# Weight buffers of their own for the merge gates, the first pair's loads beside the attention gate, and the casts of the late weights' high parts on ScalarE

## The chip, the core and the metric

The kernel runs on one core of a Trainium2 chip. The core has a matrix engine (TensorE, "PE" in the profile, with the loading of its weights as "PEld"), VectorE ("DVE"), ScalarE ("ACT"), GpSimd ("POOL"), and a sync engine ("SP") that in this kernel issues every transfer between HBM and the on-chip memory. Each engine works through its own instructions in order and waits at semaphores for the others. The metric is the device time of one execution in microseconds (us).

## The reference

One inference step of a decoder layer: a prompt of 1024 tokens and eight single tokens, 1032 columns in all, go through one combined projection into two gated branches, whose sum is projected once more. Cut to what matters here:

```python
def project(x, c, pos, p):
    h = rmsnorm(x, p['g_pre']) * (1 + scale) + shift
    z = h @ p['w_in']
    zq, zkv, zg, za, zconv, zcg, zm = jnp.split(z, ...)
...
def finish(x, o_attn, conv_out, pr, p):
    ya = (o_attn * jax.nn.silu(pr['a_gate'])) @ p['w_br_a']
    yb = (pr['cb'] * conv_out * jax.nn.silu(pr['cgate'])) @ p['w_br_b']
    ga, gb = jnp.split(jax.nn.sigmoid(pr['merge']), 2, axis=-1)
    o = (ga * ya + gb * yb) @ p['w_out']
    return x + pr['gate'] * rmsnorm(o, p['g_post'])
```

`a_gate` (`za`, 512 columns of `w_in`) is the attention gate, `merge` (`zm`, 2048 columns) the merge gates of the two branches. The width of the model is 1024, that of the branches 512.

## The kernel before

**Arithmetic.** Each float32 operand of a matmul is split in two parts: a high part, cast to TensorE's own 32-bit type, and a low part, which is the rest. A product takes three matmuls: high by high, high by low, low by high. `Hh` and `Hl` are the parts of the normed input, `wh` and `wl` those of a weight. Tokens run along the free dimension, 1032 of them: in thirds of 344 (`CH`) in the projections and in quarters of 258 (`HS`) in the merge gates.

**Weights.** The class `Weights` (object `W`) holds a list of weight tiles of 128x512, the items, in the order of their use. `load` brings an item into `wraw`, `do_split` casts it to `wh` (line 182, through `copy`, lines 110 or 112) and makes `wl` (line 183, through `sub`, line 115); `get` hands the pair out. Each of the three has three buffers, so an item can be split as soon as the third one before it is released by the last matmul that reads it. `W.hi` and `W.lo` name the engine of the two steps: at first `W.hi` is ScalarE (`A`); line 1109, at the end of attention, puts both on VectorE (`V`).

**Stages, in order of time in the trace.** The attention and its filling work end near 583 us. The last quarter of the convolution (`conv_tiles(3, ...)`, loop with `YH` and `YL`) follows to 635. Then comes branch b's projection `yb`, eight items by three thirds, to 690 (loop at line 1303; its results go to HBM in `ybd`). The attention gate (loop `for j in range(4)`, `e_za`) takes 690 to 735.3: eight items of `W`; ScalarE makes a tanh (line 1351) and the high part `oh`, VectorE multiplies and makes `ol`, and both go to HBM in `oad`. Beside it VectorE makes sums of the input's halves for the stage after (`sums14`, line 1335). The merge gates, eight pairs of 128-column blocks, run from 735.3 to 918, then branch a's projection to 964 (here `w_out` comes in as `wor` and is split to `WOh` and `WOl`), and the output to 1069.

**The merge gates.** A pair (class `Pair`) takes the 2x2 products of blocks of weights and input by a scheme with seven products in place of eight: the operands are a11, a12, a22 as loaded and the sums s1 = a21 + a22, s2 = s1 - a11, s3 = a11 - a21, s4 = a12 - s2. `load` brings the four blocks of 256 KB into buffers `ra` (six of them, in the pool `gsp`, line 1400), `total` makes the sums on VectorE into `wraw` (lines 1263 and 115), `prepare` makes `wh` on ScalarE and `wl` on VectorE, and `product` issues 24 matmuls, 12 for each half of 258 columns. a11's results are copied to `c1` by ScalarE, VectorE adds them to those of s2 and s3 (`u2`, `u3`, line 1263), and sums on VectorE and a tanh on ScalarE (`sgo`, line 1494) end it. Pair 0's a11 and a12 are the last items of `W`, loaded and split ahead. `Gate` objects, two behind each pair, use `ra` too, for blocks of `w_ada`. The eight loads of `M` bring `ybd` back.

**What sets the order.** The code's order is that of the functions; a scheduler then orders the instructions of each engine by its own estimate of when they can run, so rows of one engine stand in another order than the code. All transfers go through SP's one queue, which issues them in that order and stops where one has to wait. Pools stand on two sides of the on-chip memory, `left` and `right`, as stacks: a pool that is opened takes the place of one that was closed, and its first writers wait for the last readers of what lay there. `gsp` opens at line 1373, after the gate's pool `tp` is closed; pools that opened before it stay below.

## Time and profile before

| | us |
|---|---|
| three runs | 1069.9, 1070.4, 1072.63 |
| median | 1070.4 |
| profiled execution, its own time | 1071.21 |
| its span in the trace | 1069.2 |
| TensorE busy | 1021.5 |
| VectorE busy | 727.9 |
| ScalarE busy | 545.6 |

The profile is of one execution; its span is 2.0 us shorter than that execution's own time, and 0.8 us of that time is what it lies above the median of the runs. Times in the trace count from the span's start. Engines overlap, so the busy times don't add up to the span. In a timeline a row can stand for several like instructions (xN), and what stands in brackets is how long the engine was idle ahead of it and what ended that. Matmuls are pipelined: the time of one is longer than the distance between two.

### The profile page before, as it was taken

How to read it: one execution, taken by the hardware profiler on the slowest of the kernel's cores; microseconds unless marked ns; L12 is line 12 of the kernel's file. 1: busy time of each engine (PE TensorE's matmuls, PEld its weight loads, DVE VectorE, ACT ScalarE, POOL GpSimd, SP SyncE). 2: the span in 40 equal slices, each digit the busy share in tenths (PEclk: the TensorE clock that was granted, in tenths of full speed). 3: DMA queues.
4: the chain of work that ended last, by engine and by line, in shares of the span. 5: the costliest groups of instructions: out<-in, count | busy, mean ns of one | idle time of the engine just before them, and what ended most of it. 6: DMA issues, size and time to landing. Idle time of an engine off the chain costs nothing.

```text
span 1069.2 us, 18057 instructions
## 1 busy us (share of the span) xinstructions
PE 1021.5 (96%) x6526; PEld 940.3 (88%) x6526; DVE 727.9 (68%) x1920; ACT 545.6 (51%) x1198; POOL 94.0 (9%) x98
## 2 busy tenths in 40 slices
PE   5899999989999999999999999997899999999997
PEld 4689999978888888988898999997899999997786
DVE  4677656458887888878888748494666676785433
ACT  4566533347888877888777214232344444222221
POOL 2100000122232112220111010000000000000000
PEclk9899999989999999999999999999899999999999
DMA  9752243210111011010101363345734422873222
GB/s 315 232 145 84 62 103 77 77 45 22 35 30 26 16 25 30 21 30 11 26 11 44 98 199 115 114 142 167 237 109 120 119 70 100 264 224 113 80 79 78
DMA packets 117178, 104.15 MB, mean 97 GB/s; under 512 B 25443, under 2 KB 101674, under 8 KB 117090
## 3 DMA queue, kind: packets, MB, share of 16 engines
q1 hardware_dynamic: 117090, 103.02, 32.6%
q8 instruction: 51, 0.84, 0.3%
q14 instruction: 37, 0.30, 0.1%
HBM read 79.13 MB, written 21.76 MB: 94 GB/s over the span
## 4 chain that ended last, share of the span: by engine, by line
PE 77%; DVE 10%; ACT 4%; issue 2%; DMA 1%; SPq 1%; POOL 1%; POOLq 0%; DVEq 0%; ACTq 0%
PE psacc L106 36%; PE psS L106 23%; PE psO L106 6%; PE psT L106 5%; PE psT L1016 5%; DVE P L961 2%; DVE P L987 2%; ACT P L966 1%; DVE pl L115 1%; SPq L91 1%; DMA ra<-w_in 1%; ACT ph L110 1%; PE psT L1028 1%; DVE sm L975 1%; PE psT L570 1%
## 5 line engine op out<-in xcount | busy, mean ns | idle before, releaser
L106 PE MATMUL psacc<-Hh,wh 128*128 128x344 f32 (+1 forms) x816 | 262.0, 321 | 4.1 <-DVE Hh L112 3.8
L106 PE MATMUL psacc<-Hl,wh 128*128 128x344 f32 (+1 forms) x816 | 258.0, 316 | 0.9 <-DVE ss L329 0.7
L106 PE MATMUL psacc<-Hh,wl 128*128 128x344 f32 (+1 forms) x816 | 257.3, 317 | 0.1
L106 PEld LDWEIGHTS psacc<-Hh,wh 128*128 128x128 f32 x816 | 154.2, 189 | 12.9 <-DVE Hh L112 3.9
L106 PEld LDWEIGHTS psacc<-Hl,wh 128*128 128x128 f32 x816 | 154.1, 189 | 6.0 <-DVE Hl L115 2.6
L106 PEld LDWEIGHTS psacc<-Hh,wl 128*128 128x128 f32 x816 | 153.5, 189 | 2.4 <-DVE wl L115 1.1
L966 ACT ACTIVATE P<-P,mx 128x64 f32<-128x64 f32 (+5 forms) x192 | 115.1, 600 | 34.7 <-DVE mx L961 33.1
L115 DVE TENSOR_TENSOR pl<-psT,ph 128x512 fp32r<-128x512 f32 x132 | 90.4, 687 | 24.5 <-ACT ph L110 24.1
L110 ACT ACTIVATE wh<-wraw 128x512 fp32r<-128x512 f32 x94 | 58.8, 627 | 84.8 <-PE psS L106 37.1
L1016 PE MATMUL psT<-ident,P 128*128 128x128 f32 x528 | 89.9, 280 | 9.1 <-DVE P L987 7.1
L115 DVE TENSOR_TENSOR wl<-wraw,wh 128x512 fp32r<-128x512 f32 x98 | 67.3, 688 | 41.3 <-ACT wh L110 39.7
L110 ACT ACTIVATE ph<-psT 128x512 fp32r<-128x512 f32 x132 | 77.9, 591 | 28.6 <-PE psT L1016 24.6
L961 DVE CUSTOM_DVE_ANT_0 P<-psS,kbig 128x64 f32<-128x64 f32 (+4 forms) x192 | 74.2, 407 | 20.2 <-PE psS L106 19.4
L1016 PEld LDWEIGHTS psT<-ident,P 128*128 128x128 f32 x528 | 63.7, 141 | 26.9 <-DVE P L987 10.7
L106 PE MATMUL psS<-K,qh 128*128 128x384 f32 (+6 forms) x208 | 67.4, 327 | 2.2 <-DVE mx L961 1.2
L106 PE MATMUL psS<-K,ql 128*128 128x384 f32 (+6 forms) x208 | 68.3, 329 | 0.0
L115 POOL TENSOR_TENSOR wl<-wraw,wh 128x512 fp32r<-128x512 f32 x28 | 37.1, 1326 | 275.5 <-ACT wh L110 263.4
L106 PE MATMUL psO<-pl,V 128*128 128x512 f32 x132 | 60.8, 461 | 0.0
L106 PE MATMUL psO<-ph,V 128*128 128x512 f32 x132 | 52.4, 397 | 0.0
L961 DVE CUSTOM_DVE_ANT_0 P<-psS,kbig,mx 128x256 f32<-128x256 f32 (+3 forms) x80 | 41.9, 524 | 9.4 <-PE psS L106 8.2
L106 PEld LDWEIGHTS psS<-K,qh 128*128 128x128 f32 x208 | 39.4, 189 | 4.9 <-DMA qh<-qh 1.3
L1613 POOL TENSOR_TENSOR fst<-fst,mhalf 128x1 f32<-128x1 f32 (+1 forms) x9 | 4.9, 549 | 422.5 <-DVE fst L1612 422.5
(392 smaller groups left out, 2351.3 us busy)
## 6 DMA issues: line engine op xcount, KB each, us to landing
wraw<-w_in SPq DMA_DIRECT2D x46, 256.0 KB
ra<-w_in SPq DMA_DIRECT2D x32, 256.0 KB
ybd<-yb SPq DMA_DIRECT2D x24, 172.0 KB
M<-ybd SPq DMA_DIRECT2D x8, 516.0 KB
sgd<-sgo SPq DMA_DIRECT2D x8, 516.0 KB
OA<-oad SPq DMA_DIRECT2D x6, 688.0 KB
sg<-sgd SPq DMA_DIRECT2D x8, 516.0 KB
x<-x_prompt SPq DMA_DIRECT2D x8, 512.0 KB
```

Of the source, the lines that this page charges most:

```text
L91: return nc.sync.dma_start(out, in_)
L106: PE.matmul(out, lhsT, rhs, start=start, stop=stop, skip_group_check=True)
L110: A.activation(out, in_, AF.Copy)
L115: eng.tensor_tensor(out=out, in0=a, in1=b, op=OP.subtract)
L570: PE.transpose(pt[:, t * 128:(t + 1) * 128], raw[:, (t0 + t) * 128:(t0 + t + 1) * 128], ident)
L961: V.tensor_tensor_reduce(out=Pb[:, j, o:o + n], in0=ps[:, c0:c0 + n], in1=m, scale=1.0, scalar=init, op0=OP.add, op1=OP.min, accum_out=mx[ ...
L966: A.activation(Pb[:, j, 0:total_n], Pb[:, j, 0:total_n], AF.Exp, bias=mx[:, j, ci % 2:ci % 2 + 1], scale=-1.0, accum_out=sm[:, 0, x, j:j + 1])
L975: V.tensor_tensor(out=fac, in0=fac, in1=gt_[:, b0:b0 + np_, :], op=OP.mult)
L987: V.tensor_scalar(p, p, f[:, jj:jj + 1], None, op0=OP.mult)
L1016: PE.transpose(pt[:, j * 128:(j + 1) * 128], u.P[u.br][:, j, n * 128:(n + 1) * 128], ident)
L1028: PE.transpose(pt[:64, j * 128:(j + 1) * 128], u.P[0][:, j, :], ident)
L1613: P.tensor_tensor(out=st[:n, 3:4], in0=st[:n, 3:4], in1=mhalf[:n], op=OP.pow)
```

## The change

It does three things.

- Line 1109 sets `W.lo` alone. `W.hi` stays what it was in attention, ScalarE, so the casts of the high parts of all later items of `W` are ScalarE's: the last of the convolution, branch b, the attention gate, a11 and a12 of pair 0, and branch a. By the counts of instructions, 32 casts `wh<-wraw` leave VectorE.
- The `ra` buffers, six as before, move from the pool `gsp` to a pool `rap` of their own, which opens ahead of the gate's pool `tp`. `Gate.prepare` takes its tile from there too.
- The loads of pair 0 are written ahead of the loop of the attention gate (`raw0`); those of the other pairs stay where they were.

```diff
--- before.py
+++ after.py
@@ -1106,7 +1106,7 @@
         product()
     for _ in filler:
         pass
-    W.lo, W.hi = V, V
+    W.lo = V
     actx.close()
     att.close()
 
@@ -1322,6 +1322,19 @@
 
     tsp4 = pool("tsp4", "left", tsctx)
     T4 = [tsp4.tile([128, 4, HT], F32R, name=f"T4{x}") for x in "hl"]
+    rap = pool("rap", "left", tsctx)
+
+    def raw_tile():
+        return rap.tile([128, 4, 128], F32, name="ra", tag="ra", bufs=6)
+
+    def load_raw(c0):
+
+        raw = {}
+        for x, i, kh in (("a11", 0, 0), ("a21", 1, 0), ("a22", 1, 1), ("a12", 0, 1)):
+            raw[x] = raw_tile()
+            dma(raw[x], w_in[:, 4 * kh:4 * kh + 4, c0 + 128 * i:c0 + 128 * i + 128])
+        return raw
+
     tctx = ExitStack()
     tp = pool("tp", "left", tctx)
     zt = {x: [tp.tile([128, CH], d, name=x, tag=x, bufs=b) for _ in range(b)] for x, d, b in
@@ -1345,6 +1358,7 @@
             yield
 
     making = sums14()
+    raw0 = load_raw(GA0)
     for j in range(4):
         def e_za(c, acc, cs):
             t, oh, ol = spare("zt", F32, 3), spare("oh", F32R, 2), spare("ol", F32R, 2)
@@ -1379,9 +1393,6 @@
     def gtile(name, n, bufs):
         return fresh[name].pop(0) if fresh[name] else gp.tile([128, n], F32, name=name, tag=name, bufs=bufs)
 
-    def operand(c0, kh):
-        return w_in[:, 4 * kh:4 * kh + 4, c0:c0 + 128]
-
     RIGHT = {"a11": lambda k: quarter(k, 0), "a12": lambda k: quarter(k + 4, 0), "s1": lambda k: quarter(k, 1),
              "s4": lambda k: quarter(k + 4, 1)}
     for n, t in (("s2", T2), ("s3", T3), ("a22", T4)):
@@ -1395,10 +1406,7 @@
             self.raw, self.ops = {}, {}
 
         def load(self):
-            c0 = (GB0 if self.gb else GA0) + 128 * self.f
-            for x, (i, kh) in (("a11", (0, 0)), ("a21", (1, 0)), ("a22", (1, 1)), ("a12", (0, 1))):
-                self.raw[x] = gp.tile([128, 4, 128], F32, name="ra", tag="ra", bufs=6)
-                dma(self.raw[x], operand(c0 + 128 * i, kh))
+            self.raw = load_raw((GB0 if self.gb else GA0) + 128 * self.f) if self.n else raw0
 
         def total(self, x):
             if x in self.raw:
@@ -1504,7 +1512,7 @@
             self.b, self.k = n // KT, n % KT
 
         def prepare(self, q):
-            r = gp.tile([128, 512], F32, name="ra", tag="ra", bufs=6)
+            r = raw_tile().rearrange("p k c -> p (k c)")
             dma(r, wada[:, self.k, 2048 + 512 * self.b:2560 + 512 * self.b])
             h = wp.tile([128, 512], F32R, name="wh", tag="wh", bufs=3)
             l = wp.tile([128, 512], F32R, name="wl", tag="wl", bufs=3)
```

What it does to the order of SP's queue, first in the kernel before, around the end of the attention gate (`oad` are the gate's writes; `M` the loads for later pairs; `ra_8603` to `ra_8609` pair 0's blocks; `ra_8653` and `ra_8655` the first two of pair 1):

```order
L91 DMA oad1_7410<-ol_8521 128x344 [waits DMAHW0_49,DVE_49]
L91 DMA M_8585<-ybd_7412 128x1032 [waits DMAHW1_49,DVE_49,PE_49]
L91 DMA oad0_7409<-oh_8563 128x344 [waits DMAHW2_49,Activation_49]
L91 DMA oad1_7410<-ol_8564 128x344 [waits DMAHW3_49,DVE_49]
L91 DMA M_8585<-ybd_7412 128x1032 [waits DMAHW4_49]
L91 DMA M_8585<-ybd_7412 128x1032 [waits DMAHW5_49]
L91 DMA ra_8603<-w_in 128x4x128 [waits DMAHW6_49,PE_49]
L91 DMA ra_8605<-w_in 128x4x128 [waits DMAHW7_49]
L91 DMA ra_8607<-w_in 128x4x128 [waits DMAHW0_49]
L91 DMA ra_8609<-w_in 128x4x128 [waits DMAHW1_49]
L91 DMA ra_8653<-w_in 128x4x128 [waits DMAHW2_49]
L91 DMA ra_8655<-w_in 128x4x128 [waits DMAHW3_49]
```

Here pair 0's four blocks and two of pair 1 stand behind the gate's last writes and three loads of `M`. In the changed kernel, around the end of branch b and the start of the gate (`ybd` are branch b's last writes, `wraw` the gate's items; `ra_8081` to `ra_8087` are pair 0's blocks, `ra_8656` and `ra_8658` the first two of pair 1):

```order
L91 DMA ybd_7412<-yb_8013 128x344 [waits DMAHW0_49,Activation_49]
L91 DMA ybd_7412<-yb_8033 128x344 [waits DMAHW1_49,Activation_49]
L91 DMA ra_8081<-w_in 128x4x128 [waits DMAHW2_49,PE_49]
L91 DMA ra_8083<-w_in 128x4x128 [waits DMAHW3_49]
L91 DMA ybd_7412<-yb_8049 128x344 [waits DMAHW4_49,Activation_49]
L91 DMA ra_8085<-w_in 128x4x128 [waits DMAHW5_49]
L91 DMA ra_8087<-w_in 128x4x128 [waits DMAHW6_49]
L91 DMA wraw_8179<-w_in 128x4x64 [waits DMAHW7_49,DVE_49]
L91 DMA wraw_8179<-w_in 128x4x64 [waits DMAHW0_49]
L91 DMA ra_8656<-w_in 128x4x128 [waits DMAHW1_49]
L91 DMA ra_8658<-w_in 128x4x128 [waits DMAHW2_49]
```

These six blocks now stand between branch b's last writes and behind the gate's first item. And the changed kernel at the end of the gate, where SP had three loads of `M` ahead of pair 0's (`ra_8660` and `ra_8662` are the last two of pair 1):

```order
L91 DMA oad0_7409<-oh_8574 128x344 [waits DMAHW7_49,Activation_49]
L91 DMA ra_8660<-w_in 128x4x128 [waits DMAHW0_49,DVE_49]
L91 DMA oad1_7410<-ol_8575 128x344 [waits DMAHW1_49,DVE_49]
L91 DMA ra_8662<-w_in 128x4x128 [waits DMAHW2_49]
L91 DMA ra_8788<-w_ada 128x512 [waits DMAHW3_49,DVE_49]
L91 DMA M_8596<-ybd_7412 128x1032 [waits DMAHW4_49]
L91 DMA M_8596<-ybd_7412 128x1032 [waits DMAHW5_49]
L91 DMA M_8596<-ybd_7412 128x1032 [waits DMAHW6_49]
```

So six of the first eight blocks have moved from behind the gate to ahead of it; the other two stand around the gate's last write, and `M` stands behind them and behind a block of `w_ada`.

ScalarE around the end of the gate, before (`zt` is the gate's tanh, `oh` its high part, `c1` the copies of a11's results, `wh_8615` the high part of s2, `wh_8649` of s3, `wh_8687` of s1):

```order
L110 ACTIVATE Hh_87<-t1_8077 128x516 [waits PE_49]
L1351 ACTIVATE zt_8562<-psacc_8529 128x344 [waits PE_49]
L1354 ACTIVATE oh_8563<-zt_8562 128x344 [waits DMAHW5_49,DVE_49,Activation_49]
L110 ACTIVATE c1_8592<-psacc_8619 128x258 [waits PE_49,Activation_49]
L110 ACTIVATE c1_8593<-psacc_8620 128x258 [waits PE_49]
L1494 ACTIVATE sgo_8590<-psacc_8619 128x258 [waits DMAHW3_49,DMAHW2_49,DMAHW4_49,DMAHW0_49,DMAHW6_49,DVE_49,PE_49]
L1494 ACTIVATE sgo_8590<-psacc_8620 128x258 [waits PE_49]
L110 ACTIVATE wh_8615<-wraw_8611 128x512 [waits DVE_49]
L110 ACTIVATE wh_8649<-wraw_8647 128x512 [waits DVE_49]
L110 ACTIVATE wh_8687<-wraw_8612 128x512
```

The three high parts of pair 0's sums stand behind `c1` and the first two `sgo`. ScalarE there in the changed kernel (`wh_8569` belongs to a12 of pair 0, `wh_8618` to s2, `wh_8652` to s3, `wh_8690` to s1):

```order
L1368 ACTIVATE oh_8531<-zt_8530 128x344 [waits DMAHW1_49,DVE_49,Activation_49]
L110 ACTIVATE wh_8569<-wraw_8442 128x512 [waits DMAHW2_49,PE_49]
L110 ACTIVATE Hh_87<-t1_8080 128x516 [waits PE_49]
L110 ACTIVATE wh_8618<-wraw_8614 128x512 [waits PE_49]
L1365 ACTIVATE zt_8573<-psacc_8540 128x344 [waits PE_49]
L1368 ACTIVATE oh_8574<-zt_8573 128x344 [waits DMAHW3_49,DVE_49,Activation_49]
L110 ACTIVATE wh_8652<-wraw_8650 128x512 [waits DVE_49,PE_49]
L110 ACTIVATE wh_8690<-wraw_8615 128x512 [waits PE_49,Activation_49]
L110 ACTIVATE c1_8603<-psacc_8622 128x258
L110 ACTIVATE c1_8604<-psacc_8623 128x258
L1502 ACTIVATE sgo_8601<-psacc_8622 128x258 [waits DMAHW2_49,DMAHW1_49,DMAHW4_49,DMAHW0_49,DMAHW6_49,DVE_49,PE_49]
```

The high part of s2 has moved from behind the first `sgo` to ahead of the gate's last tanh, and those of s3 and s1 to ahead of `c1`; the one of s1 waits for a buffer that TensorE leaves.

VectorE at the same place, before (`wraw_8612` is s1's sum, `wraw_8611` s2's, `wraw_8647` s3's, `wraw_8749` s4's):

```order
L1352 SCALAR_TENSOR_TENSOR zt_8562<-zt_8562,psacc_8529 128x344 [waits Activation_49]
L115 TENSOR_TENSOR Hl3_418<-t1_8077,Hh_87 128x516
L1353 TENSOR_TENSOR zt_8562<-zt_8562,QO_871 128x344 [waits DVE_49]
L1355 SCALAR_TENSOR_TENSOR ol_8564<-zt_8562,oh_8563 128x344 [waits DMAHW6_49,Activation_49]
L1263 TENSOR_TENSOR wraw_8612<-ra_8605,ra_8607 128x512 [waits DMAHW7_49,DMAHW0_49]
L115 TENSOR_TENSOR wraw_8611<-wraw_8612,ra_8603 128x512 [waits DMAHW6_49,DVE_49]
L115 TENSOR_TENSOR wraw_8647<-ra_8603,ra_8605 128x512
L115 TENSOR_TENSOR wl_8616<-wraw_8611,wh_8615 128x512 [waits PE_49,Activation_49]
L115 TENSOR_TENSOR wl_8650<-wraw_8647,wh_8649 128x512 [waits PE_49,Activation_49]
L115 TENSOR_TENSOR wl_8688<-wraw_8612,wh_8687 128x512 [waits PE_49,Activation_49]
L115 TENSOR_TENSOR wraw_8749<-ra_8609,wraw_8611 128x512 [waits DMAHW1_49,DVE_49]
L1263 TENSOR_TENSOR u2_8594<-psS_8691,c1_8592 128x258 [waits PE_49]
```

All of pair 0's sums and low parts stand behind the gate's last row, `ol_8564`. VectorE there in the changed kernel (s1's and s2's sums, `wraw_8615` and `wraw_8614`, stand 15 rows or more further ahead; `wraw_8867` is the first sum of pair 1):

```order
L1366 SCALAR_TENSOR_TENSOR zt_8573<-zt_8573,psacc_8540 128x344 [waits Activation_49]
L115 TENSOR_TENSOR wl_8619<-wraw_8614,wh_8618 128x512 [waits PE_49]
L1367 TENSOR_TENSOR zt_8573<-zt_8573,QO_871 128x344 [waits DVE_49]
L115 TENSOR_TENSOR wraw_8650<-ra_8081,ra_8083 128x512
L1369 SCALAR_TENSOR_TENSOR ol_8575<-zt_8573,oh_8574 128x344 [waits DMAHW4_49,Activation_49]
L115 TENSOR_TENSOR wl_8653<-wraw_8650,wh_8652 128x512 [waits PE_49,Activation_49]
L115 TENSOR_TENSOR wraw_8752<-ra_8087,wraw_8614 128x512 [waits DVE_49]
L1263 TENSOR_TENSOR wraw_8867<-ra_8658,ra_8660 128x512 [waits DMAHW0_49,DVE_49]
L115 TENSOR_TENSOR wl_8691<-wraw_8615,wh_8690 128x512 [waits PE_49,Activation_49]
L1263 TENSOR_TENSOR u2_8605<-psS_8694,c1_8603 128x258 [waits Activation_49]
L1263 TENSOR_TENSOR u2_8606<-psS_8695,c1_8604 128x258 [waits Activation_49]
```

What stood behind the gate's last multiply now stands before or between its steps; and the first sum of pair 1, which waits for a load (`ra_8660`), has come to stand ahead of s1's low part and of both `u2`.

## Rows read from the trace of the kernel before

**Rows 1.** The profile's page: busy time of each engine with its share of the span and its instructions, and the granted clock of TensorE in 40 equal slices of the span, in tenths.

```profile
PE 1021.5 (96%) x6526; PEld 940.3 (88%) x6526; DVE 727.9 (68%) x1920; ACT 545.6 (51%) x1198; POOL 94.0 (9%) x98
...
PEclk9899999989999999999999999999899999999999
```

**Rows 2.** Waits of TensorE from 575 to 735 us: engine, tile and line, what it waited for, us in total, times, longest us.

```profile
PE psacc L106 <- ACT YH L110: 0.7, 1, 0.7
PE psT L1161 <- DVE sP L1155: 0.6, 2, 0.4
```

**Rows 3.** Waits of all engines from 735 to 770 us, same columns.

```profile
DVE wraw L1263 <- DMA ra<-w_in: 10.1, 1, 10.1
...
PE psS L106 <- ACT wh L110: 9.3, 1, 9.3
...
ACT wh L110 <- DVE wraw L115: 6.7, 1, 6.7
```

**Rows 4.** The chain of waits from 735 to 770 us, in order of time: start us, us, what.

```profile
736.46 0.42 DVE zt L1352
...
738.39 0.38 ACT c L110
...
741.71 7.43 DMA ra<-w_in
...
749.17 0.70 DVE wraw L1263
...
751.26 0.04 issue
751.30 8.45 PE psS L106 x48
759.75 2.90 PE psT L106 x24
```

**Rows 5.** A table of stretches: from and to, us, then busy us (and instructions) of PE, PEld, DVE, ACT and POOL, the granted clock as a share of full, the share of the DMA engines, GB/s.

```profile
620.00:640.00 20.00, 19.32 (x133) 18.91 (x133) 7.04 (x16) 2.99 (x6) 2.78 (x3) 1.00 0.79 252
...
741.96:751.30 9.34, 0.01 (x1) 0.00 (x0) 2.00 (x4) 1.34 (x4) 0.00 (x0) 0.74 1.10 333
751.30:760.00 8.70, 8.70 (x52) 8.70 (x53) 5.77 (x11) 1.98 (x4) 0.00 (x0) 0.69 0.80 249
...
769.31:790.66 21.35, 21.35 (x174) 20.59 (x174) 12.91 (x24) 8.99 (x20) 0.00 (x0) 1.00 0.42 123
```

**Rows 6.** Timeline of SP's queue from 734 to 760 us: start us, us, engine, line, operation, out<-in, xcount.

```profile
737.98 0.32 SPq L91 DMA_DIRECT2D M<-ybd  x1
...
739.44 1.01 SPq L91 DMA_DIRECT2D M<-ybd  x2
740.54 6.59 SPq L91 DMA_DIRECT2D ra<-w_in  x6
```

**Rows 7.** Transfers issued from 690 to 800 us: out<-in, queue, operation, count, KB of one.

```profile
M<-ybd SPq DMA_DIRECT2D x8, 516.0 KB
ra<-w_in SPq DMA_DIRECT2D x16, 256.0 KB
```

**Rows 8.** Timeline of TensorE, at the end of the gate and the start of pair 0, and at the start of pair 1.

```profile
734.67 0.32 PE L106 MATMUL psacc<-Hh,wl 128*128 128x344 f32 x1
...
735.30 0.28 PE L106 MATMUL psacc<-Hh,wh 128*128 128x258 f32 x1
...
736.94 0.39 PE L106 MATMUL psacc<-Hh,wh 128*128 128x258 f32 x1
...
738.82 0.39 PE L106 MATMUL psacc<-Hh,wh 128*128 128x258 f32 x1 [0.16 <-ACT c L110]
...
769.15 0.29 PE L106 MATMUL psacc<-Hh,wh 128*128 128x258 f32 x1
```

**Rows 9.** Groups of instructions by line and shape, the casts of 128x512 weights' high parts: busy us, mean ns of one | idle us before them, and what ended most of it.

```profile
L110 ACT ACTIVATE wh<-wraw 128x512 fp32r<-128x512 f32 x94 | 58.8, 627 | 84.8 <-PE psS L106 37.1 <-PE psacc L106 25.4 <-issue 14.5
...
L112 DVE CAST wh<-wraw 128x512 fp32r<-128x512 f32 x32 | 13.7, 428 | 20.0 <-PE psS L106 9.6 <-PE psacc L106 9.1 <-DMA wraw<-w_br_a 1.3
```

**Rows 10.** Timeline of VectorE from 754 to 762 us.

```profile
754.72 0.43 DVE L1263 TENSOR_TENSOR u<-psS,c 128x258 f32<-128x258 f32 x1 [0.94 <-PE psS L106]
...
760.38 0.69 DVE L115 TENSOR_TENSOR wl<-wraw,wh 128x512 fp32r<-128x512 f32 x1 [0.17 <-ACT wh L110]
```

**Rows 11.** Timeline of SP's queue from 925 to 945 us, loads of `w_out` blocks of 128x512.

```profile
929.51 0.93 SPq L91 DMA_DIRECT2D wor<-w_out  x2
...
938.92 0.33 SPq L91 DMA_DIRECT2D wor<-w_out  x1
```

**Rows 12.** Timeline of ScalarE from 930 to 944 us, the copies that wait for these loads.

```profile
932.47 1.33 ACT L110 ACTIVATE WOh<-wor 128x512 fp32r<-128x512 f32 x2 [3.45 <-DMA wor<-w_out]
...
943.11 0.63 ACT L110 ACTIVATE WOh<-wor 128x512 fp32r<-128x512 f32 x1 [3.43 <-DMA wor<-w_out]
```

**Rows 13.** Timeline of ScalarE at the end of attention and at the end of the convolution.

```profile
567.69 0.60 ACT L110 ACTIVATE ph<-psT 128x512 fp32r<-128x512 f32 x1 [0.41 <-PE psT L1016]
...
634.58 0.46 ACT L874 ACTIVATE ct<-psacc 128x344 f32<-128x344 f32 x1 [3.32 <-PE psacc L106]
```

**Rows 14.** Timeline of VectorE from 634 to 636.5 us.

```profile
634.36 0.43 DVE L112 CAST wh<-wraw 128x512 fp32r<-128x512 f32 x1 [0.48 <-PE psacc L106]
...
635.50 0.51 DVE L875 SCALAR_TENSOR_TENSOR ct<-ct,psacc 128x344 f32<-128x344 f32 x1
```

## The prediction

> **What bounds the kernel now.** I read the page first. TensorE is busy 96% of the span and its clock is at full in nearly every slice [rows 1], so a change can gain only where TensorE stands still or runs slowly. Next come the waits of TensorE. From 575 to 735 us, which holds the last convolution, the second branch's projection and the attention gate, it waited for another engine in two places, 0.7 and 0.6 us [rows 2]. From 735 to 770 us it waited 9.3 us once, for ScalarE's copy of a weight's high part; ScalarE waited 6.7 us for VectorE's sums, and VectorE 10.1 us for the load of `ra` [rows 3]. The chain tells the same in order of time: 7.43 us of `ra` load, a sum of 0.70 us and a second like it, one copy, then matmuls from 751.30 [rows 4]. The stage table has the price: 9.34 us with no matmul at a granted clock of 0.74, and after it 8.70 us at 0.69 [rows 5].
>
> Why the load is late: the queue issued it at 740.54, with three loads of `M` in front of it (737.98 and 739.44, the second row is two) [rows 6], of 516 KB each where `ra` has 256 [rows 7]. VectorE's first sum began at 749.17 [rows 4], 8.6 us behind the issue.
>
> What the place costs in all: pair 0 starts its first matmul at 735.30 and pair 1 at 769.15 [rows 8], 33.85 us. A pair without a stall, from 769.31 to 790.66, takes 21.35 us at clock 1.00 [rows 5]. The excess is **12.50 us**. It splits into 9.34 us idle; the 48 matmuls from 751.30, which take 8.45 us where 24 at full clock behind them take 2.90 [rows 4], so 8.45 - 2 x 2.88 = 2.69 us of slow clock; the rest, 0.47 us, lies ahead of 736.94 and 738.82, to which 12 matmuls each took 1.64 and 1.88 us [rows 8] in place of 1.45. (24 in 2.90 us is 0.12 us a matmul; 2.88 is 24 x 0.12.)
>
> **Part 1: buffers of their own, the first pair's loads early.** In the changed order the four loads of pair 0 and two of pair 1 stand between the last writes of `yb`, some 45 us before their first use. 1.5 MB in that stretch lies beside a stage in which TensorE waits for no load, so I cost it at nothing; the cover is those 45 us. The sums for s1 and s2 are ahead of the gate's last group on VectorE, and s2's copy stands right behind the last `Hh` copy on ScalarE. Its buffer is free when the gate's last matmul ends at 735.30; one copy is 0.63 us [rows 9], so it ends near 736.0, and the first half of a11 keeps TensorE until 735.30 + 12 x 0.12 = 736.74. The 9.34 us go, and with them the slow clock: an idle of 0.7 us at 637 us left the clock of 620 to 640 us at 1.00 [rows 2, 5].
>
> What is late next, by the order of the changed kernel:
> - TensorE takes the first s1 matmuls straight behind s2, and s1's high part goes into the buffer that s2 leaves. So one copy stands open: 0.63 us [rows 9] and two hand-overs of 0.04 us as in the chain [rows 4], **0.7 us**. Lower bound 0, if the buffer is another; upper 1.6 us, if both copies of `c1` behind it on ScalarE (0.35 and 0.38 us, as the chain's 0.38 [rows 4]) are also waited for.
> - The last multiply of the gate on VectorE must free the bank for a11's second half. ScalarE's tanh before it comes one copy later, but four s2 matmuls stand in front of that half. I take 0.
> - Pair 1's third load must wait for s3's sum, since its buffer is a11's or a21's. The gate's last multiply was at 736.46 [rows 4]; with its 0.42 us, s2's low part (0.69), a second multiply like it and s3's sum (0.70) that is 738.7, and up to 0.63 more by the copy ahead of the tanh: I take 739.2. VectorE's sum for pair 1 waits for the load, and behind that sum stand s1's low part and the two sums `u2` that free the bank for s3. s3 is due near 735.30 + 3 x 2.88 + 4 x 0.12 + 0.7 = 745.1; 0.70 + 0.69 + 0.43 us of VectorE work lie between [rows 4, 10], so the load must be there by 743.3, 4.1 us after its issue. Loads of the same 256 KB took 3.0 us (929.51 to 932.47) and 4.2 us (938.92 to 943.11) from issue to the copy that waits for them [rows 11, 12]; the far end is the 8.6 us above. The nearest is 3.0, with no large load in front, which `M` no longer is. I take 0; the far end costs 739.2 + 8.6 + 1.8 - 745.1 = 4.5 us.
> - `M` is loaded behind all this, during pair 0, and is first used by pair 4. The first `sgo` on ScalarE waits for the gate's last write; behind it stands a22's copy, due near 735.30 + 5 x 2.88 = 749.7. Nothing.
>
> The Trainium skill ("DMA: Bandwidth & Descriptors", section "Queues, rings and completion order") says that on each DMA engine the descriptors of one queue are taken in ring order. The 8.6 us behind three loads of `M` agree; by that rule the load of pair 1, with one write of the gate in front, lands in time, and the sum stays.
>
> **Part 2: high parts on ScalarE.** 32 casts leave VectorE (0.428 us each, 13.7 us) and come to ScalarE (0.627 us each, 20.1 us) [rows 9]. Neither is the bound: ScalarE is busy 51%, VectorE 68% [rows 1]. The casts on VectorE waited 9.6 and 9.1 us for TensorE to leave a buffer [rows 9], so they come early by nature: three items are ahead, and a buffer left in the middle of an item's last third is needed 12 or more matmuls later, 1.9 us. One cast costs 0.20 us more on ScalarE, and VectorE then waits for ScalarE. Both fit in 1.9 us, so I take 0 for all but two.
> - At the end of attention one copy goes in front of `ph` at 567.69, before which ScalarE stood 0.41 us [rows 13]. 0.63 less 0.41 leaves 0.2 us, of which some meets TensorE: 0.1, between 0 and 0.6.
> - At the end of the convolution the second cast (634.36) comes in front of the tanh at 634.58 [rows 13, 14], whose chain ends in TensorE's 0.7 us wait for `YH` [rows 2]. The multiply at 635.50 already stood behind that split on VectorE [rows 14]. 0.1, between 0 and 0.4.
> - In the first branch's projection the copies stand between those of `w_out` on ScalarE, which wait for loads; TensorE is never idle there and each is due an item later (36 matmuls, four in 0.63 us before 735.30 [rows 8]: 5.7 us). 0. VectorE with 13.7 us less may free a bank sooner: 0, or a gain of up to 0.5.
>
> The Trainium skill ("ScalarE: Activation LUTs", section "Rules for kernel authors") advises simple elementwise work on VectorE, not on ScalarE. The 0.428 against 0.627 us agree with it, so it speaks against this part; what it would make of the time is the rival on ScalarE below.
>
> **Sum.** -12.5 + 0.7 + 0.2 = **-11.6 us**. The profiled execution had a span of 1069.2 and a time of 1071.2, so 1057.6 and 1059.6 there; from the median of 1070.4 it is **1058.8 us**. The bounds alone: best -12.5 - 0.5 = -13.0 (1057.4), worst -12.5 + 1.6 + 4.5 + 1.0 = -5.4 (1065.0).
>
> **Rivals.**
> - *The wait moves to pair 1's load.* If it lands as late as before, VectorE holds s1's low part and `u2` until 749.6 and TensorE stands 4.5 us before s3, perhaps at a slower clock after it (8.70 us at 0.69 cost 2.69, so half of that: 1.3). 1058.8 + 4.5 to 5.8: 1063.3 to 1064.6. For it: the 8.6 us. Against it: no `M` in front.
> - *ScalarE's queue becomes the wait: slower.* ScalarE works in order, so a cast can stand behind an evacuation that waits for TensorE. Each of the 32 exposed would cost 0.20 us of length, 0.17 us of hand-over (VectorE's wait for `wh` at 760.38 [rows 10]) and an evacuation of 0.46 us [rows 13]: 0.83 x 32 = 27 us, or 1085. It decides the sign from 11.6 / 32 = 0.36 us each. Against it: two waits of TensorE in 160 us [rows 2], and the early release. A small part of it, 0.12 us each or 4 us in all, would give 1063.
> - *The loads don't come early.* The new buffers lie where the branch stage's operands were, so the first waits for TensorE to end that stage. If the queue were held to the end of the gate, nothing is gained: 1070 to 1071. Against it: the order has them between the last `yb` writes, which that same TensorE work releases.
>
> **How the numbers follow.** Forecast (1057.4 to 1061): 0.76. More gain than the bound: 0.03. Part of the casts exposed (1061 to 1063.5): 0.07. Pair 1's load (1063 to 1065): 0.08. No early loads: 0.03. ScalarE slower: 0.03. The likeliest gives 1058.8. To hold 8 in 10 the range takes the forecast, a little below its best bound and the partly exposed casts: 1056.8 to 1063.0. A measurement here can tell about 0.3% (3.2 us), so under 1067.2 is faster: 0.94; within: 0.03; slower: 0.03.
>
> **What would show it.** After the gate no idle of TensorE over 1.5 us, and a clock of 1.00 through pair 0, which should last 22 us. `ra` issued near 690 us; `M` behind pair 1's loads. No cast of `wh` on VectorE, some 20 us more on ScalarE. TensorE's waits from 575 to 735 us still near 1.3 us. Wrong if VectorE waits for `ra` before s3, if the clock falls in pair 0, or if TensorE waits for `wh` many times in the branch stages.

## The result and the profile after

The changed kernel takes 1060.74 us (1059.99 to 1061.38, four runs), the kernel before beside it 1071.32 (1069.90 to 1072.63, four runs): a ratio of 0.9901, 95% interval 0.9884 to 0.9918. In a second set of five runs it took 1059.46 beside 1071.0: 0.9900, 0.9886 to 0.9914. So by the medians it is faster by 10.6 and 11.5 us; the forecast was 11.6 less, 1058.8, in a range of 1056.8 to 1063.0. The profiled execution has a span of 1059.4 us.

The page, beside [rows 1]: 32 instructions and 10.5 us have left VectorE, 17.5 us have come to ScalarE, and the one slice of the late half in which the clock was below full is at 9 now.

```profile
PE 1020.5 (96%) x6526; PEld 936.9 (88%) x6526; DVE 717.4 (68%) x1888; ACT 563.1 (53%) x1230; POOL 94.1 (9%) x98
...
PEclk8899999999999999999999999999999999999999
```

The group of casts, beside [rows 9]: one row, where there were two. By this row ScalarE's casts are 20.2 us more, which the forecast had as some 20.

```profile
L110 ACT ACTIVATE wh<-wraw 128x512 fp32r<-128x512 f32 x126 | 79.0, 628 | 109.3 <-PE psS L106 43.6 <-PE psacc L106 42.4 <-issue 16.3
```

Waits of TensorE from 570 to 780 us, beside [rows 2, 3] (engine, tile and line, what it waited for, us in total, times, longest). The wait of 9.3 us for `wh` is gone, one of 0.7 us has come.

```profile
PE psT L106 <- ACT wh L110: 0.7, 1, 0.7
PE psacc L106 <- ACT YH L110: 0.6, 1, 0.6
PE psT L1161 <- DVE sP L1155: 0.2, 1, 0.2
```

TensorE's timeline, beside [rows 8]: pair 0 begins at 736.75, resumes behind that wait at 743.42, comes to s3 at 746.87, and pair 1 begins at 758.82. Pair 0 lasts 22.07 us where it lasted 33.85.

```profile
736.75 0.28 PE L106 MATMUL psacc<-Hh,wh 128*128 128x258 f32 x1
...
743.42 0.39 PE L106 MATMUL psT<-Hh,wh 128*128 128x258 f32 x1 [0.66 <-ACT wh L110]
...
746.87 0.28 PE L106 MATMUL psS<-T3h,wh 128*128 128x258 f32 x1
...
758.82 0.30 PE L106 MATMUL psacc<-Hh,wh 128*128 128x258 f32 x1
```

The stretches of pair 0, and pair 1 behind it, beside [rows 5] (from and to, us, then busy us of PE, PEld, DVE, ACT and POOL, clock, DMA share, GB/s). The clock column is the thing to read: 1.00 in each, also behind the idle of 0.66 us.

```profile
736.75:742.76 6.01, 6.00 (x50) 5.77 (x48) 5.39 (x10) 2.13 (x6) 0.00 (x0) 1.00 0.36 100
742.76:743.42 0.66, 0.00 (x1) 0.00 (x1) 0.00 (x0) 0.66 (x2) 0.00 (x0) 1.00 1.12 365
743.42:750.00 6.58, 6.58 (x54) 6.58 (x55) 3.72 (x8) 1.90 (x6) 0.00 (x0) 1.00 0.98 333
750.00:758.86 8.86, 8.86 (x73) 8.29 (x72) 5.78 (x12) 4.38 (x10) 0.00 (x0) 1.00 1.03 367
758.86:780.30 21.44, 21.44 (x174) 20.69 (x174) 13.00 (x24) 9.06 (x20) 0.00 (x0) 1.00 0.54 161
```

The chain through that place, beside [rows 4] (start us, us, what): matmuls, one copy, matmuls. No load stands in it.

```profile
740.37 2.29 PE psS L106 x19
...
742.74 0.64 ACT wh L110
...
743.42 0.74 PE psT L106 x4
744.16 2.87 PE psacc L106 x24
```

SP's queue, beside [rows 6]: six `ra` between 691.73 and 697.8, the third block of pair 1 at 740.65, and the first `M` only behind it.

```profile
691.73 0.94 SPq L91 DMA_DIRECT2D ra<-w_in  x2
...
693.29 1.05 SPq L91 DMA_DIRECT2D ra<-w_in  x2
...
695.58 2.19 SPq L91 DMA_DIRECT2D ra<-w_in  x2
...
740.65 0.39 SPq L91 DMA_DIRECT2D ra<-w_in  x1
...
742.84 1.37 SPq L91 DMA_DIRECT2D M<-ybd  x3
```

VectorE beside it: the first sum of pair 1 waited 1.90 us for that block and began 3.66 us behind its issue; the two `u2` ended at 746.28, 0.6 us ahead of s3.

```profile
744.31 0.69 DVE L1263 TENSOR_TENSOR wraw<-ra 128x512 f32<-128x512 f32 x1 [1.90 <-DMA ra<-w_in]
...
745.52 0.76 DVE L1263 TENSOR_TENSOR u<-psS,c 128x258 f32<-128x258 f32 x2
```

Where the time went, by stages. The table is worked out from TensorE's timeline of each trace: A is the start of the attention's first matmul with the keys `K`, B the first matmul of pair 0, C the first of branch a, D the last of all; each column is a difference. The first two rows are the kernels of this section, the others the experiments below.

| run | to A | A to B | B to C | C to D |
|---|---|---|---|---|
| before | 231.72 | 503.58 | 183.12 | 144.32 |
| after | 233.37 | 503.38 | 171.36 | 144.88 |
| a1_after_again | 231.02 | 503.43 | 171.36 | 144.38 |
| e1_buffers_only | 232.38 | 503.61 | 171.46 | 144.71 |
| e2_casts_only | 231.74 | 503.51 | 183.12 | 144.45 |
| e3_written_late | 232.00 | 503.39 | 171.40 | 144.37 |
| e4_no_m | 230.81 | 503.58 | 177.65 | 144.30 |
| e6_own_s1 | 232.26 | 503.48 | 171.70 | 144.92 |
| e7_cast_twice | 231.00 | 504.14 | 173.03 | 148.29 |
| e8_load_twice | 230.35 | 503.64 | 171.63 | 144.37 |
| e9_held | 231.55 | 503.42 | 171.38 | 144.38 |
| e10_held_twice | 231.46 | 503.23 | 173.98 | 144.38 |
| e11_c1_first | 232.19 | 503.51 | 170.45 | 144.37 |

The whole gain is in B to C, the pairs: 11.76 us. It is in pair 0 alone: from one pair's first matmul to the next one's (for the last pair to C), pairs 1 to 7 take 21.27 to 21.37 us each in all thirteen traces, but for the last one of e7, of which more below. Up to A all these kernels are alike, and yet that takes 230.35 to 233.37 us; the profiled executions of the two kernels happen to lie 1.65 us apart there, so their spans differ by 9.8 us only. The two A rows, of before and of after:

```profile
231.72 0.36 PE L106 MATMUL psS<-K,qh 128*128 128x192 f32 x1 [1.06 <-DMA qh<-qh]
```

```profile
233.37 0.35 PE L106 MATMUL psS<-K,qh 128*128 128x192 f32 x1 [1.06 <-DMA qh<-qh]
```

### The profile page after: what moved, and what is told of

Same layout as the page of the kernel before. It is cut to its first block, busy times and chain, and to the rows that moved or that the text cites. A ratio compares the mean times of both kernels' runs of the same rounds, so it can differ in the third digit from the quotient of the medians.

```text
span 1059.4 us, 18075 instructions
## 1 busy us (share of the span) xinstructions
PE 1020.5 (96%) x6526; PEld 936.9 (88%) x6526; DVE 717.4 (68%) x1888; ACT 563.1 (53%) x1230; POOL 94.1 (9%) x98
## 4 chain that ended last, share of the span: by engine, by line
PE 79%; DVE 8%; ACT 3%; issue 2%; DMA 1%; SPq 1%; POOL 1%; POOLq 0%; DVEq 0%; ACTq 0%
PE psacc L106 37%; PE psS L106 23%; PE psO L106 6%; PE psT L1016 5%; PE psT L106 5%; DVE P L961 2%; DVE P L987 2%; ACT P L966 1%; SPq L91 1%; DVE pl L115 1%; DMA OA<-oad 1%; ACT ph L110 1%; PE psT L1028 1%; DVE sm L975 1%; PE psT L570 1%
## 5 line engine op out<-in xcount | busy, mean ns | idle before, releaser
L106 PEld LDWEIGHTS psacc<-Hh,wh 128*128 128x128 f32 x816 | 154.0, 189 | 11.8 <-DVE Hh L112 4.0
L110 ACT ACTIVATE wh<-wraw 128x512 fp32r<-128x512 f32 x126 | 79.0, 628 | 109.3 <-PE psS L106 43.6
L961 DVE CUSTOM_DVE_ANT_0 P<-psS,kbig 128x64 f32<-128x64 f32 (+4 forms) x192 | 74.3, 408 | 20.2 <-PE psS L106 19.3
L106 PEld LDWEIGHTS psS<-K,ql 128*128 128x128 f32 x208 | 39.7, 191 | 2.0
```

What stands on the lines that cost most here:

```text
L106: PE.matmul(out, lhsT, rhs, start=start, stop=stop, skip_group_check=True)
L110: A.activation(out, in_, AF.Copy)
L961: V.tensor_tensor_reduce(out=Pb[:, j, o:o + n], in0=ps[:, c0:c0 + n], in1=m, scale=1.0, scalar=init, op0=OP.add, op1=OP.min, accum_out=mx[ ...
```

## The experiments

**The change again, and each part alone.** This one and the next three were timed beside one another.

> The changed kernel once more, timed beside the three others of this set. If the forecast's sum holds, 11.6 us less than before: a ratio near 0.989. If the 1.0 us that the first measurement lacked against it is a real cost of the change, 0.990 to 0.991, and the trace shows that cost between the end of attention and the end of branch a; if it is the spread of single executions, it stands in stages that the change doesn't touch.

Measured: the ratio 0.9900 of above. The stages are those of the first trace, but for the one ahead of A (231.02) and the last (144.38, where the first trace had 144.88; 0.4 of that 0.5 us lie ahead of the matmul of branch a that there waited 0.2 us for a load of `OA`, which brings the gate's output `oad` back). From A to D the two traces of the changed kernel are 11.40 and 11.85 us below before. So as far as two traces can tell, the missing 1.0 us was the spread of executions, and not a cost in the stages that the change touches.

```diff
-    W.lo = V
+    W.lo, W.hi = V, V
```

> Part 1 alone: the buffers of their own, with VectorE casting the late high parts as before. Theory (the gain is the early loads, part 2 is worth nothing): the same time as the whole change within 1 us, ratio 0.989 to 0.991, one idle of TensorE of about 0.7 us in pair 0. Rival (VectorE needs the 13.7 us that part 2 takes off it, to have the sums ready beside the gate): an idle of 2 us or more in pair 0 and 1063 us or more. Rival (part 2 costs about 1 us somewhere): 1 us less than the whole change, near 1059.5.

Measured: 1060.23 us, ratio 0.9891 (0.9877 to 0.9906); B to C 171.46, one idle of 0.7 us in pair 0. VectorE with its 13.7 us of casts had the sums ready all the same. The buffers alone are the gain, and both rivals fall.

```diff
 (the kernel before)
-    W.lo, W.hi = V, V
+    W.lo = V
```

> Part 2 alone: the casts on ScalarE, the buffers and loads of the first pair where they were. Theory: no difference, ratio 0.999 to 1.001, the idle of 9.3 us before s2 still there. Rival (ScalarE's queue becomes the wait): over 1073 us, with waits of TensorE for wh in branch b, the gate and branch a. Rival (part 2 brings part of the gain): under 1068.

Measured: 1069.97 us, ratio 0.9992 (0.9983 to 1.0001), the wait where it was. Its waits from 735 to 770 us:

```profile
DVE wraw L1263 <- DMA ra<-w_in: 10.1, 1, 10.1
...
PE psS L106 <- ACT wh L110: 9.3, 1, 9.3
```

Part 2 is worth nothing that the timing can tell. Pieces of A to B, read in the same way, tell a little more. From A to the attention's last matmul of `pl` (the low parts of its weights) with the values `V` it took 350.17 to 350.21 us in the three traces with VectorE's casts (before, e1, e4), and 350.21 to 350.57, with a median of 350.42, in nine with ScalarE's (both of the changed kernel, e2, e3, e6, e8 to e11): some 0.2 us lost at the median, nothing in e10. No wait of TensorE shows where. From there to the last matmul of branch b it was 108.02 to 108.04 in the three and 107.64 to 107.69 in the nine: 0.4 us won.

**What cover the casts have.**

```diff
             copy(self.hi, h, r)
+            if self.lo is V and self.nsp >= LATE:
+                copy(self.hi, h, r)
...
     W.lo = V
+    LATE = W.nsp
```

> The changed kernel with each late high part cast twice over on ScalarE: 32 casts of 0.63 us more, 20 us of ScalarE work. The forecast says that a cast has 1.9 us of cover at least. Theory: within 1 us of the changed kernel, as two casts and a hand-over (1.4 us) still fit. Rival (the casts of the changed kernel stand just at the edge of their cover): 32 x 0.3 to 0.6 = 10 to 20 us more, with many waits of TensorE for wh or wl.

Measured: 1064.28 us, ratio 0.9936 (0.9924 to 0.9949), by the medians 4.8 us over the changed kernel. Between the two, then. The single traces differ by more, 6.3 us from A to D against a1. Of these 0.7 us lie ahead of pair 0: 0.5 by the end of the attention (350.91 us to the same matmul of `pl`), where TensorE waits 0.2 us for `pl` as in no other trace, and 0.2 from there to the end of branch b, where the wait for `YH` at the end of the convolution is 1.1 us in place of 0.6. The others, 1.7 and 3.9, lie on either side of C, where the merge gates give way to branch a. TensorE's rows there, and the stretch behind them:

```profile
906.27 0.40 PE L106 MATMUL psO<-wl,cA 128*9 128x512 f32 x1
908.17 0.89 PE L106 MATMUL psacc<-OA,wh 128*128 128x344 f32 x4 [1.50 <-ACT wh L110]
911.26 0.42 PE L106 MATMUL psS<-OA,wh 128*128 128x344 f32 x1 [2.19 <-DMA OA<-oad]
```

```profile
911.26:920.00 8.74, 8.74 (x46) 8.74 (x47) 1.38 (x3) 3.25 (x6) 0.00 (x0) 0.80 0.78 237
```

ScalarE's rows there (`gm` is the result of the `Gate` objects):

```profile
905.66 1.15 ACT L110 ACTIVATE wh<-wraw 128x512 fp32r<-128x512 f32 x2 [0.34 <-PE psT L106]
906.72 0.40 ACT L1501 ACTIVATE ct<-ct 128x258 f32<-128x258 f32 x1
907.03 0.57 ACT L110 ACTIVATE gm<-psO 18x512 f32<-18x512 f32 x1
907.51 1.14 ACT L110 ACTIVATE wh<-wraw 128x512 fp32r<-128x512 f32 x2
```

The row at 905.66 holds the first casts of branch a's first two weights. Their second casts came to stand behind the last pair's tanh and the copy of `gm`, at 907.51, and TensorE, through with the pairs at 906.5, waited 1.50 us for the first of them. So at this place the scheduler made 1.5 us of wait out of the 0.63, and nothing is told of its cover. Behind it stands a wait of 2.19 us for `OA`. That load was not late: its issue at 903.18 is 5.0 us ahead of C, where a1's is 3.3 us ahead, and it took 8.0 us as the like one took 7.7 in the first trace of the changed kernel. TensorE came to it early, with the fifth matmul of branch a, where that is the 25th in before, after, a1 and e1. And behind the two waits the clock is 0.80 for 8.74 us; at full speed 0.80 of that time would do, so some 1.7 us by estimate, and 2.2 + 1.7 are the 3.9 behind C. So these 5.6 us stand at one place, and in the orders that the scheduler made there. Elsewhere, but for the ends of the attention and of the convolution, a second cast found room: TensorE shows no other wait for `wh` than the 0.7 us in pair 0.

**Which half of the change brings the loads early.**

```diff
-    raw0 = load_raw(GA0)
     for j in range(4):
...
+    raw0 = load_raw(GA0)
     mp = pool("mp", "right")
```

> The changed kernel with the loads of pair 0 written behind the loop of the attention gate, the buffers of their own kept. Theory (it is the buffers that let the loads go early; the place in the code only sets numbers): the loads still issue near 692 us, ratio 0.989 to 0.991. Rival (the place in the code brings them early): issued behind the gate, an idle of several us in pair 0, 1065 us or more.

Measured: 1059.94 us, ratio 0.9898 (0.9881 to 0.9914), the first `ra` issued at 690.37. The place in the code made no difference here; the scheduler put the load where its buffer let it, and the buffers are the change.

**What the 9.3 us were made of.**

```diff
-                    dma(M[:, f, :], yb_d[f])
+                    P.memset(M[:, f, :], 0.0)
```

> The kernel before without its eight loads of M; GpSimd fills M with zeros instead, so branch b's part is missing from the output. This separates the late issue of ra behind the gate from the 1.5 MB of M in front of it. Theory (most of the 8.6 us from issue to the first sum was M): ra issues at 738, lands in 3 to 4 us, the first sum is near 742 and s2 starts near 743.5; TensorE is idle some 2 us instead of 9.3, the clock stays at 1.00, the time is 9 to 11 us less, 1060 to 1062. Rival (the place behind the gate alone costs it, and ra takes 8 us in any case): idle of 6 us or more, 1066 to 1070.

Measured: 1064.97 us, ratio 0.9947 (0.9929 to 0.9964), about half of the gain; by B to C it is 5.5 of the 11.8 us. The waits from 734 to 770 us, SP's row, VectorE's first sum, and the stretches of and behind the idle:

```profile
DVE wraw L1263 <- DMA ra<-w_in: 5.5, 1, 5.5
...
PE psS L106 <- ACT wh L110: 4.7, 1, 4.7
```

```profile
738.57 8.04 SPq L91 DMA_DIRECT2D ra<-w_in  x8
```

```profile
743.64 0.69 DVE L1263 TENSOR_TENSOR wraw<-ra 128x512 f32<-128x512 f32 x1 [5.51 <-DMA ra<-w_in]
```

```profile
741.04:745.78 4.74, 0.01 (x2) 0.01 (x1) 2.01 (x4) 1.07 (x3) 3.43 (x4) 1.00 1.04 272
745.78:750.00 4.22, 4.22 (x22) 4.22 (x23) 3.42 (x6) 1.07 (x2) 0.00 (x0) 0.60 0.57 151
750.00:753.36 3.36, 3.36 (x30) 3.36 (x30) 2.14 (x5) 0.66 (x2) 0.00 (x0) 1.00 0.28 76
```

Without `M` the queue came to `ra` 4.18 us behind pair 0's start at 734.39 (before 5.24), and the first sum followed 5.07 us behind the issue (before 8.63). So `M` made 4.6 of the 9.3 us of idle, and the place behind the gate, with eight blocks in one row here, the other 4.7. An estimate agrees: three loads of 128x1032 floats are 1.59 MB, and at the 333 GB/s of the idle before [rows 5] they take 4.8 us. I had expected 3 to 4 us for the landing and 2 us of idle, and a clock of 1.00; the landing was of several blocks at once, and an idle of 4.74 us left the clock at 0.60 for the next 4.22 us. Both theories were half right. GpSimd's zeros ran beside it (7.27 us of GpSimd from 737.20), with VectorE's sums at 0.69 us as ever.

**The price of pair 1's load.**

```diff
-            dma(raw[x], w_in[:, 4 * kh:4 * kh + 4, c0 + 128 * i:c0 + 128 * i + 128])
+            for _ in range(2 if c0 == GA0 + 256 and x == "a22" else 1):
+                dma(raw[x], w_in[:, 4 * kh:4 * kh + 4, c0 + 128 * i:c0 + 128 * i + 128])
```

> The changed kernel with the third block of pair 1 loaded twice in a row into the same buffer, the second time behind the first one's landing. This delays the load of the first rival by about 4 us. Theory (VectorE holds s1's low part and u2 behind the sum that waits for this load, with 0.6 us to spare in the trace of the changed kernel): TensorE idle 3 to 4 us before s3, the time 3 to 5 us more than the changed kernel, 1063.5 to 1066. Rival (the scheduler or another buffer keeps that wait off the path): no idle there, the same time. The clock after the idle is read too: 9.3 us of idle left 0.69 behind it.

Measured: 1058.51 us, ratio 0.9887 (0.9869 to 0.9904): no cost that the timing can tell; pair 0 lasts 22.37 us, 0.3 more than in the changed kernel. But VectorE's rows show that the theory wasn't tried:

```profile
741.27 0.75 DVE L1263 TENSOR_TENSOR u<-psS,c 128x258 f32<-128x258 f32 x2
746.35 0.69 DVE L1263 TENSOR_TENSOR wraw<-ra 128x512 f32<-128x512 f32 x1 [4.33 <-DMA ra<-w_in]
```

The scheduler had seen the second load and put both `u2` (741.27) ahead of the sum that waits for it (746.35). The sum's place in front of `u2` is its choice, and the wait came off the path with another one. So I held the order, by a copy of one column of the block into `u2` ahead of the sums:

```diff
+                if self.n == 0 and s == 0:
+                    V.tensor_copy(self.u2[0][:, 0:1], pairs[1].raw["a22"][:, 0, 0:1])
                 add(self.u2[s], ps, self.c1[s])
```

> The changed kernel with VectorE held to the order of the first rival: a copy of one column out of pair 1's third block into u2 stands ahead of the two sums u2, which so can't be taken before that load is there. Control for the next one. Theory (in the changed kernel VectorE waited 1.9 us for this load and had 0.6 us left to s3): no idle of TensorE before s3, the time of the changed kernel within 1 us. Rival (the margin is not there in most executions): an idle of 0.3 to 1 us before s3.

Measured: 1059.56 us, ratio 0.9897 (0.9881 to 0.9914), B to C 171.38, no idle ahead of s3.

> As before, and the third block of pair 1 loaded twice. Without the hold the scheduler had moved the waiting sum behind u2, and the double load cost nothing; there the second load was in 12.4 us behind pair 0's first matmul, and s3 was due at 10.6. Theory (the first rival's mechanism, with its price): u2 ends 13.2 us behind pair 0's start, TensorE idle some 2.5 us before s3, the clock after it perhaps at half for some us (1 to 2 us more): 2.5 to 4.5 us more than the control. Rival (s3 doesn't wait for u2's bank): the control's time.

Measured: 1061.44 us, ratio 0.9913 (0.9896 to 0.9930), 1.9 us over the control; B to C 173.98, 2.6 over it. VectorE's copy and its two sums, TensorE's rows, and the stretches of and behind the idle:

```profile
746.74 0.15 DVE L1482 COPY u<-ra 128x1 f32<-128x1 f32 x1 [4.70 <-DMA ra<-w_in]
746.81 0.75 DVE L1263 TENSOR_TENSOR u<-psS,c 128x258 f32<-128x258 f32 x2
```

```profile
745.18 0.28 PE L106 MATMUL psacc<-Hh,wl 128*128 128x258 f32 x1
747.28 0.72 PE L106 MATMUL psS<-T3h,wh 128*128 128x258 f32 x2 [1.81 <-DVE u L1263]
```

```profile
745.46:747.28 1.82, 0.01 (x2) 0.00 (x1) 0.54 (x3) 0.83 (x2) 0.00 (x0) 1.00 0.96 337
747.28:751.00 3.72, 3.72 (x29) 3.58 (x30) 2.81 (x6) 0.38 (x1) 0.00 (x0) 1.00 0.77 274
```

The mechanism is there: `u2` late by the load, s3 late by `u2` (1.81 us). The idle of 1.82 us left the clock at 1.00, so the price is at the lower end of my 2.5 to 4.5, or under it by the timing. Not all of the 2.6 us is this wait: pair 0 is 0.3 longer in e8 too, which has the second load without the hold, and in both TensorE takes six of s1's matmuls ahead of a12's where the changed kernel and e9 take four. Some 0.5 is not accounted for.

**What is left in pair 0.**

```diff
+            if self.n == 0 and x == "s1":
+                h = gp.tile([128, 4, 128], F32R, name="ws", tag="ws", bufs=1)
+            else:
+                h = wp.tile([128, 4, 128], F32R, name="wh", tag="wh", bufs=3)
...
-                t = tmp("ct", 5)
+                t = tmp("ct", 4)
...
```

> The changed kernel with a buffer of its own for the high part of s1 in pair 0 (one of the ct buffers given up for the room). Theory (the 0.7 us left in pair 0 is the copy that waits for s2's buffer): no idle of TensorE over 0.3 us in pair 0, which lasts 21.4 us; the time 0.7 us less, a ratio 0.0006 lower, which the timing can hardly tell but the trace can. Rival (the wait moves to VectorE's low part or to c1): an idle of 0.3 to 1 us at another place of pair 0.

Measured: 1060.73 us, ratio 0.9905 (0.9891 to 0.9919), B to C 171.70, 0.3 more than the changed kernel. The rival held. ScalarE's rows, and the matmul that waits:

```profile
741.72 0.63 ACT L110 ACTIVATE wh<-ra 128x512 fp32r<-128x512 f32 x1 [1.77 <-PE psS L106]
742.26 0.65 ACT L110 ACTIVATE c<-psacc 128x258 f32<-128x258 f32 x2
```

```profile
742.68 0.39 PE L106 MATMUL psacc<-Hh,wh 128*128 128x258 f32 x1 [0.94 <-ACT c L110]
```

TensorE now took a12 behind s2, and a12 adds to the banks that `c1` is copied from. `c1` stood on ScalarE behind another cast that waits for s2's buffer, a22's. So it is not one buffer, it is that any waiting cast holds `c1`. The last kernel gives s1 the buffer and a22's cast to VectorE:

```diff
 (on top of the one before)
-            copy(A, h, self.raw[x])
+            copy(V if self.n == 0 and x == "a22" else A, h, self.raw[x])
```

> The changed kernel with a buffer of its own for s1's high part in pair 0 and a22's high part there cast by VectorE, so that no cast that waits for TensorE stands ahead of the copies c1 on ScalarE, and a12 can follow s2 at once. Theory (what is left in pair 0 is ScalarE's queue: c1 behind a cast that waits for s2's buffer): the idle of 0.7 to 0.9 us between s2 and a12 goes. s3 then is due 0.7 us earlier, within 0.2 us of u2 behind pair 1's load, so 0 to 0.4 us can come back there; pair 0 lasts 21.4 to 21.8 us, 0.3 to 0.7 us off the time, under what the timing can tell. Rival (it is the buffer alone): the idle stays.

Measured: 1058.37 us, ratio 0.9883 (0.9866 to 0.9899). Pair 0 has no idle left and lasts from 735.70 to 756.86, 21.16 us; B to C is 0.91 us under the changed kernel. VectorE still waits for pair 1's block, and `u2` stands right behind:

```profile
735.70 0.28 PE L106 MATMUL psacc<-Hh,wh 128*128 128x258 f32 x1
...
756.86 0.30 PE L106 MATMUL psacc<-Hh,wh 128*128 128x258 f32 x1
```

```profile
742.98 0.69 DVE L1263 TENSOR_TENSOR wraw<-ra 128x512 f32<-128x512 f32 x1 [0.92 <-DMA ra<-w_in]
743.58 0.75 DVE L1263 TENSOR_TENSOR u<-psS,c 128x258 f32<-128x258 f32 x2
```

It is the best of the kernels by its median and by its trace; the intervals of it and of the changed kernel overlap, so the timing alone doesn't tell them apart (e8 has 1058.51 with a longer pair 0).

## Why the prediction was right, point by point

**The excess of 12.50 us and its end.** Right, in place and size: pair 0 lost 11.78 us (33.85 to 22.07), where the forecast had 12.5 less 0.7, 11.8. The clock behind the place is at 1.00, as forecast. That part 1 alone does it is shown by e1, and that it is the buffers and not the place in the code by e3.

**Nothing for the early loads.** Right: the gate's stage is 45.37 us in the trace after and 45.36 before, with 1.5 MB more in it.

**One copy open, 0.7 us.** Right in size (0.66 us idle). The reason given was half of it: s1's high part does wait for s2's buffer, but a buffer of its own (e6) moved the idle to `c1`, and only both together (e11) ended it. The copies of `c1`, which the forecast had as an upper bound, are the second lock behind the first.

**Pair 1's load.** Right, by less than it looked. Issue 3.90 us behind pair 0's start, as forecast (739.2 - 735.3); landing to the sum 3.66 us, between the 3.0 and the 4.2 of [rows 11, 12]; 0.6 us to spare. The rival is a true mechanism (e10), which with the landing of before would have cost 4.5 us by the forecast's own sum. Why that was so long is shown by e4: the 8.6 us were 5.1 for the blocks themselves and 3.5 for `M` in front.

The Trainium skill ("DMA: Bandwidth & Descriptors", section "Queues, rings and completion order") has descriptors of one queue taken in ring order on each engine. The 5.07 us without `M` and the 8.63 with it agree.

**Part 2 at 0.2 us.** The sum is right within what can be told (0.9992, 0.9983 to 1.0001), its terms are not, and that they nearly cancel is luck. The term at the end of attention was some 0.2 us at the median and not 0.1, inside its range of 0 to 0.6. The one at the end of the convolution, +0.1, was of the wrong sign: the wait for `YH` fell from 0.7 to 0.6 us, and from the end of attention to the end of branch b 0.4 us were won. The waits give the rest of it: TensorE waited 0.6 us there for VectorE's `sP`, a tile of the single tokens' attention [rows 2], and 0.2 us after. I had looked for such a gain in branch a alone.

**Both steps fit in 1.9 us.** Right where it was worked out, too general beyond. With a second cast at each of the 32 places (e7) TensorE waited for none in branch b and the gate, so 1.3 us and a hand-over do fit there. At the end of the convolution the second cast showed, with 0.5 us in the wait for `YH`, and at the end of attention with some 0.5 us too: there the cover is that of ScalarE's queue and not 1.9 us. These are the two places that the forecast had set apart. For the first weight of branch a the run tells nothing.

The Trainium skill ("ScalarE: Activation LUTs", section "Rules for kernel authors") gives `relu`, `max`, `min`, `add` and `mul` to VectorE and not to ScalarE; a cast is not in that row. The cast here is in line with it, 0.63 us on ScalarE and 0.43 on VectorE, and yet it made no difference that the timing can tell which engine took them; the measurement decides.

**From 11.6 to 10.6 us.** The forecast was made against a median of 1070.4; with a fourth run the kernel before was at 1071.3. The rest lies within the spread ahead of A, 3.0 us over the thirteen traces, which is about the bound of 0.3%. All of it is there at VectorE's 101st instruction, which starts between 65.3 and 68.3 us; what makes it was not tried.

## What to carry to other kernels

Where a load stands late in a queue, ask what its buffer overlaps before asking where it is written: here the same six buffers, in a pool that opens one stage earlier, let the scheduler issue the loads 45 us ahead, and it made no difference that the line that asks for them was written behind that stage (e3). Price a stall with the clock behind it, as here 9.3 us of idle and 2.7 us of slow matmuls. And when a wait is removed by giving one operand a buffer, read the queue of the engine that fills it for what stands behind the next waiting instruction.

## What the runs showed that I had not expected

- What idle times left of the clock. Behind 0.66 and 1.82 us it was 1.00; behind 4.74 us, in which it was still at 1.00, it was 0.60 for 4.22 us; behind 9.34 us, with 0.74 in the idle itself, it was 0.69 for 8.70 us [rows 5]. Two waits of 1.50 and 2.19 us with 0.9 us of matmuls between them (e7) left 0.80 for 8.74 us. A value between 0.50 and 1.00 is a stretch that has both levels in it, 1.2 and 2.4 GHz: from 747 to 749 us alone it was 0.50 in before and in e4, and from 741.96 to 745 us, the first third of the long idle, 1.00 in before. For the 4.74 us I had expected none of that.
- Executions of the same instructions differ by up to 3.0 us in their first 68 us, keep that difference up to A, and differ by 0.4 us between A and B (503.23 to 503.64, the double casts left out), though some of those kernels differ there. Differences of a stage can be read to some tenths of a microsecond from single traces, which the whole time can't.
- An experiment that makes a load longer can be answered by the scheduler: it saw the second load and moved the waiting sum behind other work, and the cost that was to be doubled was gone.
